# A hybrid backbone block on one Trainium2 core: attention pairs computed on 32-wide strips, keys transposed once per head pair, and filler gates split in four pieces

## The chip, the cores and the metric

The kernel runs on one core of a Trainium2 chip. Its time is device time in microseconds (us) for one execution of the whole block. A core has a matrix engine (PE, with its weight loads listed apart as PEld), a vector engine (DVE), a scalar engine (ACT), a general engine (POOL) and a sync engine (SP) that here only starts DMA transfers. Each engine takes its instructions strictly in the order of its own list and waits for the others through semaphores. "Before" is the median of three runs, 1084.16 us. A difference of 0.3% (3.25 us) or less is counted as no change.

## What is computed

One layer of a diffusion backbone: 512 latent tokens, 256 context tokens, width 1024, all in float32. A modulated RMS norm feeds one wide projection; two token mixers run on it (A: a gated delta rule, four heads; B: HGRN2, four heads; both scan in two directions, each from the final state of the context); the mixers' outputs are normed per head, gated, projected up, merged by sigmoid gates and projected out; then comes a SwiGLU feed-forward of width 2816. The two scans, per chunk:

```python
def gdn_chunk_scan(q, k, v, log_alpha, beta, s0, with_output):
    ...
    sol = lax.linalg.triangular_solve(a_mat, rhs, left_side=True, lower=True, unit_diagonal=True)
    ...
    k_end = k * jnp.exp(g_end[..., None] - g)[..., None]
    ...
    def step(s, xc):
        u_c = u_c - jnp.einsum('bhck,bhkv->bhcv', w_c, s)
        s_next = gam_end_c[..., None, None] * s + jnp.einsum('bhck,bhcv->bhkv', k_end_c, u_c)
        o = jnp.einsum('bhck,bhkv->bhcv', qg_c, s) + jnp.einsum('bhij,bhjv->bhiv', att_c, u_c)
        return s_next, o

def hgrn2_chunk_scan(q, k, v, log_f, s0, with_output):
    ...
    def step(s, xc):
        s_next = f_end_c[..., None] * s + jnp.einsum('bhck,bhcv->bhkv', k_end_c, v_c)
        pair = jnp.exp(jnp.where(incl[:, :, None], lg_c[:, :, :, None, :] - lg_c[:, :, None, :, :], -jnp.inf))
        att = jnp.einsum('bhik,bhjk,bhijk->bhij', q_c, k_c, pair)
        o = jnp.einsum('bhck,bhkv->bhcv', q_c * jnp.exp(lg_c), s) + jnp.einsum('bhij,bhjv->bhiv', att, v_c)
        return s_next, o
```

The kernel uses chunks of 128 tokens, not 64, and adds the triangular halves of both directions into one 128x128 attention matrix per chunk.

## The kernel before

**How the lists come about.** The program is written in a framework that gives every engine one fixed list of instructions, sorted by a priority that follows the order of writing. Tiles come from pools; a tag with `bufs=n` has n buffers, and an instruction that needs a buffer waits until the tile that held it n tiles ago has been read for the last time. PSUM has eight banks of 128x512 float32: two for the projections (tag `mm`), two for mixer B (`ha`), three for mixer A (`ga`), one for the filler gates (`fa`). A string, `PLAN`, says in which order pieces of the streams are written: `G0` and `G2` are mixer A's two pairs of heads, `H0` to `H3` mixer B's heads, `N` and `aT` pieces of the modulation product, `F` one filler gate, `X` the point after which the leftover gates and modulation pieces are written.

**Big products.** A weight matrix comes by DMA as `raw`. `split` makes of it a rounded part `hi` (ACT, L100) and the rest `lo` (DVE, L102); `mm3` (L110) multiplies hi by hi, hi by lo and lo by hi, three 128x512 matmuls for each 128 rows of weights. All projections, the gates and the feed-forward go this way.

**Filler gates.** There are 24 gate tiles of 128 columns. Nine are written by `gate_low` ahead of X: their matmuls (`pgate`) get a priority 1000 later than the place where they are written, so that they fall into gaps of the mixers. Each is made in two halves of four k-tiles (128x512 elements): one DMA of 256 KB, one cast, one subtraction, 12 matmuls. `hi` and `lo` of the pool `fl` have one buffer each, `raw` two; the finished gate goes by `gate_out` (an ACT copy and a DMA) to `gdram` in HBM.

**Mixer B (`hgrn`).** After its projections (`h_z`, `h_zv`) a head builds the attention matrix `AT` (128x4x128: four chunks side by side) level by level. Level 7 is the diagonal; levels 0 to 6 belong to b = 1, 2, 4, ..., 64: pairs whose tokens lie in the two halves of the same block of 2b tokens. Each level takes two exponentials on ACT (`E`, L511, and the first half of `kq`, L512), a product on DVE (L515, the second half of `kq`), `att`, and two updates of the running sums `K` and `L` on DVE. `att` multiplies for each of the four chunks all 128 keys with all 128 queries (L488, tile `pA` in a bank of `ha`), and then DVE copies with a mask only those pairs that belong to the level (L493, mask `lev`, 128 columns a level); level 7 is copied whole by ACT (L491). At the end `AT` is multiplied with the values into `po`.

**Mixer A (`gdn_pair`, two heads at once).** `gdn_front` makes convolved, normed keys `KTt` (key dimension on the partitions, six blocks of 128 tokens), queries and values. Then come decays and the matrices `N` and `aT`, and the inverse of the triangular matrices: a loop of 30 rounds on DVE (`p_o`, `p_Z`, L694 and L696) for 32-blocks, and solves with 32- and 64-wide matmuls (`pR`, `pX`, `pY`, L735 to L752; `pRb`, `pYb`, L760 to L770). Last come six steps, each for two heads and two directions; one of them (bank `pk`):

```python
                        nc.tensor.matmul(pk[:, P:2 * P], N[:, d, e, g, :], rt[:, :], start=True, stop=True)
                        u = rt
                        nc.scalar.activation(u[:, :], pk[:, P:2 * P], AF.Copy, scale=nbkv[:, g, d:d + 1])
                        ...
                            nc.tensor.transpose(pk[:, 2 * P:3 * P], KTt[:, g, :], ident)
                            nc.scalar.activation(kend[:, :], pk[:, 2 * P:3 * P], AF.Copy, scale=dec[:, d, 1, g, h:h + 1])
                            nc.tensor.matmul(pk[:, 2 * P:3 * P], kend[:, :], u[:, :], start=True, stop=True)
```

L792 is the product with `N`, L794 the ACT pass that makes `u` (named `p_s_r`, as it overwrites `rt`), L799 the transpose, L800 the ACT pass that makes `kend` (`p_s_ke`), L801 the product that updates the state, L804 (first step) the copy of the state `S`. The tag `blk` has three buffers and is used in turn by the convolution of the first two heads, the loop's tiles, the outputs `oa` and the normed outputs `on`. Other small matmuls named below: `column_sums` (L116: 128x32 weights at four column positions, one moving column).

## Time and profile before

| | |
|---|---|
| median of three runs | 1084.16 us (1082.39 to 1086.25) |
| profiled execution, its time | 1081.61 us |
| its span in the trace | 1079.6 us |
| granted PE clock, mean | 0.99 |
| PE, PEld busy | 1014.1 us (94%), 839.9 us (78%) |
| DVE, ACT busy | 656.5 us (61%), 554.5 us (51%) |
| POOL busy | 76.6 us (7%) |
| the chain that ended last, by engine | PE 60%, DVE 13%, DMA 9%, ACT 7%, issue 7% |
| moved by DMA | 122.07 MB, 113 GB/s on average |

Busy times add up each instruction's own time, overlaps within an engine counted once; matmuls are pipelined and their ends are modelled, so the distance from one start to the next says more about PE than a duration does. Each float32 matmul of the program with both operands in plain float32 leaves two records in the trace, a transpose one, and one in the hi/lo form (`mm3`) one. Three stretches of the span can be told apart: until about 95 us loads, norms and the first modulation; from 95 to 605 us both mixers, with the fillers in between; from 605 us on merge, output projection and feed-forward.

### The profile page before, as it was taken

What the parts mean: (1) busy time and instruction counts of PE and PEld (TensorE: products, weight loads), DVE (VectorE), ACT (ScalarE), POOL (GpSimd) and SP (SyncE); (2) the same over time, 40 slices, a digit from 0 to 9 for tenths busy, and PEclk for the clock granted to TensorE, in tenths of its full rate; (3) what the DMA queues carried; (4) which work ended last, traced back from release to release, by engine and by line L of the source; (5) the groups of instructions that cost most, each with busy time, mean ns of one, the idle gap of its engine ahead of it and who ended that gap; (6) DMA issues with size and microseconds to landing.
All of it is one profiled execution on the core that took longest, in us unless ns stands there. A gap on an engine that the chain in (4) does not pass through costs nothing.

```text
span 1079.6 us, 16501 instructions
## 1 busy us (share of the span) xinstructions
PE 1014.1 (94%) x6455; PEld 839.9 (78%) x6455; DVE 656.5 (61%) x1238; ACT 554.5 (51%) x1042; POOL 76.6 (7%) x133
## 2 busy tenths in 40 slices
PE   4999999979999999999999899999999999999996
PEld 2686788858897877789777688797888878888785
DVE  3336886789867967976797565776343433422524
ACT  3456578748976765887774643442222222221212
POOL 1010000320002022000201000010000000000000
PEclk8999999999999999999999999999999999999999
DMA  9953412122004213200738743455333323322222
GB/s 329 290 168 91 138 55 65 54 79 59 3 11 147 64 45 88 59 2 22 241 112 280 239 159 120 137 158 174 98 97 96 96 85 98 97 97 96 86 95 95
DMA packets 134529, 122.07 MB, mean 113 GB/s; under 512 B 5533, under 2 KB 110259, under 8 KB 134451
## 3 DMA queue, kind: packets, MB, share of 16 engines
q1 hardware_dynamic: 127715, 100.20, 29.9%
q0 software_dynamic: 4640, 17.30, 4.9%
q10 hardware_dynamic: 2096, 3.50, 0.9%
q8 instruction: 51, 0.84, 0.3%
q14 instruction: 27, 0.22, 0.1%
HBM read 110.51 MB, written 10.49 MB: 112 GB/s over the span
## 4 chain that ended last, share of the span: by engine, by line
PE 60%; DVE 13%; DMA 9%; ACT 7%; issue 7%; POOL 3%; SPq 0%; POOLq 0%; ACTq 0%; DVEq 0%
PE pf L110 20%; PE pfo L110 10%; PE pg L330 3%; PE pup L110 3%; PE h_z L110 3%; PE pgate L110 2%; DMA mwb<-in_mod_w_dram 2%; DVE lo L102 2%; DMA mwe<-in_mod_w_dram 2%; PE h_zv L110 2%; DMA ug<-gdram 1%; ACT hi L100 1%; DMA gdram<-gt 1%; PE p_s_pk L801 1%; PE g_k_zl L110 1%
## 5 line engine op out<-in xcount | busy, mean ns | idle before, releaser
L100 ACT CAST hi<-raw 128x1024 fp32r<-128x1024 f32 (+1 forms) x131 | 129.7, 991 | 279.9 <-PE pf L110 97.3
L102 DVE TENSOR_TENSOR lo<-raw,hi 128x1024 fp32r<-128x1024 f32 (+1 forms) x131 | 150.5, 1150 | 172.6 <-ACT hi L100 172.2
L110 PE MATMUL pf<-hhi,lo 128*128 128x512 f32 (+1 forms) x352 | 133.8, 380 | 0.8 <-DVE lo L102 0.8
L110 PE MATMUL pf<-hhi,hi 128*128 128x512 f32 (+1 forms) x352 | 133.8, 381 | 0.0
L110 PE MATMUL pf<-hlo,hi 128*128 128x512 f32 (+1 forms) x352 | 133.7, 380 | 0.0
L110 PEld LDWEIGHTS pf<-hhi,lo 128*128 128x128 f32 x352 | 66.2, 188 | 13.7 <-DVE lo L102 1.2
L110 PEld LDWEIGHTS pf<-hlo,hi 128*128 128x128 f32 x352 | 66.2, 188 | 12.5 <-DVE hlo L1042 0.2
L110 PEld LDWEIGHTS pf<-hhi,hi 128*128 128x128 f32 x352 | 66.1, 188 | 12.5
L110 PE MATMUL pfo<-lo,uh 128*128 128x512 f32 x176 | 68.8, 391 | 0.1
L110 PE MATMUL pfo<-hi,ul 128*128 128x512 f32 x176 | 68.5, 389 | 0.0
L110 PE MATMUL pfo<-hi,uh 128*128 128x512 f32 x176 | 67.9, 390 | 0.0
L110 PE MATMUL pgate<-hhi,lo 128*128 128x512 f32 x144 | 59.2, 412 | 6.5 <-DVE lo L102 6.5
L110 PE MATMUL pgate<-hhi,hi 128*128 128x512 f32 x144 | 59.2, 411 | 2.3 <-ACT hi L100 2.3
L110 PE MATMUL pgate<-hlo,hi 128*128 128x512 f32 x144 | 58.2, 404 | 0.0
L1098 DVE TENSOR_TENSOR sg<-sg,pf 128x512 f32<-128x512 f32 x22 | 15.1, 687 | 49.3 <-PE pf L110 49.3
L835 DVE SCALAR_TENSOR_TENSOR acc<-mwb,sc,acc 128x256 f32<-128x256 f32 x72 | 34.5, 484 | 12.4 <-DMA mwb<-in_mod_w_dram 11.2
L110 PEld LDWEIGHTS pfo<-lo,uh 128*128 128x128 f32 x176 | 33.0, 188 | 7.8 <-DVE lo L102 1.0
L110 PEld LDWEIGHTS pfo<-hi,uh 128*128 128x128 f32 x176 | 32.8, 188 | 7.4 <-ACT hi L100 0.7
L110 PEld LDWEIGHTS pgate<-hhi,lo 128*128 128x128 f32 x144 | 27.8, 193 | 13.8 <-DVE lo L102 8.9
L110 PE MATMUL h_z<-hhi,hi 128*128 128x512 f32 x96 | 38.1, 397 | 0.4 <-ACT abT L376 0.3
L110 PEld LDWEIGHTS pfo<-hi,ul 128*128 128x128 f32 x176 | 33.0, 188 | 6.8
L110 PE MATMUL h_z<-hhi,lo 128*128 128x512 f32 x96 | 38.0, 396 | 0.0
(443 smaller groups left out, 2498.3 us busy)
## 6 DMA issues: line engine op xcount, KB each, us to landing
raw<-in_ffn_w_in_dram SPq DMA_DIRECT2D x44, 512.0 KB, 3.7
raw<-in_w_in_dram SPq DMA_DIRECT2D x37, 512.0 KB, 3.7
raw<-in_ffn_w_out_dram SPq DMA_DIRECT2D x22, 512.0 KB, 3.6
mwb<-in_mod_w_dram POOLq DMA_DIRECT2D x18, 512.0 KB, 4.6
mw<-in_mod_w_dram SPq DMA_DIRECT2D x16, 512.0 KB, 6.0
mwe<-in_mod_w_dram POOLq DMA_DIRECT2D x7, 1024.0 KB, 6.1
gdram<-gt SPq DMA_DIRECT2D x24, 256.0 KB, 3.3
raw<-in_w_in_dram SPq DMA_DIRECT2D x18, 256.0 KB, 2.9
```

The costliest lines, as they stand in the source:

```text
L100: nc.scalar.copy(hi[:, :, :], raw[:, :, :])
L102: nc.vector.tensor_tensor(lo[:, :, :], raw[:, :, :], hi.bitcast(F32), op=ALU.subtract)
L110: nc.tensor.matmul(ps, a[u](k), b[v](k), start=(start and n == 0), stop=(stop and n == tot - 1))
L330: nc.tensor.matmul(pg0[i][:, :], u[:, P * i:P * i + P], v[:, d, :], start=(d == 0 and n == 0), stop=(d == KT - 1 and n == 2))
L801: nc.tensor.matmul(pk[:, 2 * P:3 * P], kend[:, :], u[:, :], start=True, stop=True)
L835: nc.vector.scalar_tensor_tensor(acc[:, :], mw[:, k - k0, :], sc[:, k:k + 1], acc[:, :], op0=ALU.mult, op1=ALU.add)
L1098: nc.vector.tensor_tensor(sg[:, :], sg[:, :], pgu[1][:, :], op=ALU.mult)
```

## The change

**Strips.** `att` no longer multiplies 128 keys by 128 queries. For levels 7 and 0 to 4 (blocks of at most 32 tokens) it multiplies, for each chunk, each 32 keys with the same 32 queries: 16 matmuls with 32x32 outputs at the four column positions of the array, all 128 rows in use. Their results stand as a strip of 128x(4x32). Level 7 is copied by ACT into a new tile `AD` (128x4x32), levels 0 to 4 by DVE under a mask of 32 columns a level. After level 4 four DVE copies move AD's diagonal blocks into `AT`. Level 5 (b = 32) multiplies 32 keys with the neighbouring 32 queries (`j ^ 1`), 16 matmuls, and four ACT copies of 32x4x32 write them straight into `AT`; level 6 does the same with 64x64, 8 matmuls and two ACT copies of 64x4x64. The mask `lev` shrinks from 128x896 to 128x160.

**Keys once per pair.** Between the inverse and the steps, for each head of a pair, six transposes of the keys go to two banks of `ga`, and two ACT copies (128x256, 128x512) bring them into `kt`, a tile with the tag `blk`; DVE makes `nbe`, the product of two small scale tables (128x12). In a step, the transpose and the pass for `kend` are gone: the pass after `N` is now `ue`, scaled by `nbe`, which goes into the state product with `kt`; `u` is made as well only where a latent chunk's output needs it (g >= 2).

**Filler gates in four pieces.** `gate_low` casts, subtracts and multiplies two k-tiles at a time (128x256); `hi` and `lo` have two buffers each, half as large. The DMAs stay two of 256 KB for each gate (tile `fraw`).

Counted over the program: ACT has 1040 instructions for 1006, DVE 1270 for 1240, PE's matmuls 5602 for 5266; POOL and SP keep their numbers, and SP's list is in the same order but for small shifts.

```diff
--- before.py
+++ after.py
@@ -24,6 +24,8 @@
 LEVELS = (1, 2, 4, 8, 16, 32, 64)
+NB = 32
+NSM = 5
@@ -37,7 +39,8 @@
     r, c = i[:, None], i[None, :]
     sq = np.concatenate(
         [(r == c), (r <= c), (r >= c), (r < c), (r > c)], axis=1).astype(np.float32)
-    lev = [(r // (2 * b) == c // (2 * b)) & (r // b != c // b) for b in LEVELS]
+    r, c = r % NB, c[:, 0:NB]
+    lev = [(r // (2 * b) == c // (2 * b)) & (r // b != c // b) for b in LEVELS[0:NSM]]
     return sq, np.concatenate(lev, axis=1).astype(np.float32)
 
@@ -142,11 +145,18 @@
         def gate_low(i, pool):
             ps = bank("fa", f"pgate{i}")
-            for k0 in (0, 4):
-                w = split([W_IN[P * k0:P * k0 + 4 * P, gcols[i]:gcols[i] + P]], 4, P, pool)
+            for k0 in range(0, KT, 2):
+                if k0 % 4 == 0:
+                    raw = pool.tile([P, 4, P], F32, name=f"fraw{i}{k0}", tag="raw", bufs=2)
+                    nc.sync.dma_start(raw[:, :, :], W_IN[P * k0:P * k0 + 4 * P, gcols[i]:gcols[i] + P].rearrange("(k p) f -> p k f", p=P))
+                part = raw[:, k0 % 4:k0 % 4 + 2, :]
+                hi = pool.tile([P, 2, P], F32R, name=f"fhi{i}{k0}", tag="hi", bufs=2)
+                nc.scalar.copy(hi[:, :, :], part)
+                lo = pool.tile([P, 2, P], F32R, name=f"flo{i}{k0}", tag="lo", bufs=2)
+                nc.vector.tensor_tensor(lo[:, :, :], part, hi.bitcast(F32), op=ALU.subtract)
                 tc.cur_priority += 1000
-                mm3(ps[:, :], [lambda k, t=t: t[:, k, :] for t in w], [lambda k, t=t: t[:, k0 + k, :] for t in lat], 4,
-                    start=(k0 == 0), stop=(k0 == 4))
+                mm3(ps[:, :], [lambda k, t=t: t[:, k, :] for t in (hi, lo)], [lambda k, t=t: t[:, k0 + k, :] for t in lat], 2,
+                    start=(k0 == 0), stop=(k0 == KT - 2))
                 tc.cur_priority -= 1000
             gate_out(i, ps, pool)
@@ -340,8 +350,8 @@
-            lev = cp.tile([P, 7 * P], U8, name="lev")
-            levf = s1.tile([P, 7 * P], F32, name="levf")
+            lev = cp.tile([P, NSM * NB], U8, name="lev")
+            levf = s1.tile([P, NSM * NB], F32, name="levf")
             nc.sync.dma_start(levf[:, :], T["lev"])
             nc.scalar.copy(lev[:, :], levf[:, :])
             mx = s1.tile([P, 4], F32, name="mx")
@@ -481,17 +491,31 @@
                     nc.vector.tensor_tensor(q[:, :], Z[:, 0:SEQ], sg[:, 0:SEQ], op=ALU.mult)
                 yield
             AT = hg.tile([P, 4, P], F32, name=n + "AT", tag="AT")
+            AD = hg.tile([P, 4, NB], F32, name=n + "AD", tag="AD")
             def att(kq, lvl):
+
+                w = 64 if lvl == 6 else NB
                 pA = bank("ha", f"{n}pA{lvl}")
                 for c in range(4):
-                    nc.tensor.matmul(pA[:, P * c:P * c + P], kq[:, 0, P * c:P * c + P], kq[:, 1, P * c:P * c + P],
-                                     start=True, stop=True)
+                    for j in range(P // w):
+                        kt0, qt0 = P * c + w * j, P * c + w * (j ^ (lvl in (5, 6)))
+                        nc.tensor.matmul(pA[w * j:w * j + w, w * c:w * c + w], kq[:, 0, kt0:kt0 + w], kq[:, 1, qt0:qt0 + w],
+                                         start=True, stop=True, tile_position=(0, w * j))
+                pAv = pA[:, 0:4 * w].rearrange("p (c i) -> p c i", i=w)
                 if lvl == 7:
-                    nc.scalar.copy(AT[:, :, :], pA.rearrange("p (c i) -> p c i", i=P))
+                    nc.scalar.copy(AD[:, :, :], pAv)
+                elif lvl < NSM:
+                    nc.vector.copy_predicated(AD[:, :, :], lev[:, NB * lvl:NB * lvl + NB].unsqueeze(1).to_broadcast([P, 4, NB]), pAv)
                 else:
-                    nc.vector.copy_predicated(AT[:, :, :], lev[:, P * lvl:P * lvl + P].unsqueeze(1).to_broadcast([P, 4, P]),
-                                              pA.rearrange("p (c i) -> p c i", i=P))
+                    for j in range(P // w):
+                        s = slice(w * j, w * j + w)
+                        nc.scalar.copy(AT[s, :, w * (j ^ 1):w * (j ^ 1) + w], pAv[s, :, :])
+                if lvl == NSM - 1:
+                    for j in range(P // NB):
+                        s = slice(NB * j, NB * j + NB)
+                        nc.vector.tensor_copy(AT[s, :, s], AD[s, :, :])
             kq = hg.tile([P, 2, SEQ], F32, name=n + "kqd", tag="kq", bufs=2)
             E = hg.tile([P, SEQ], F32, name=n + "Ed", tag="E")
@@ -772,6 +796,18 @@
 
             oa2 = gd.tile([P, 2, 4, P], F32, name=n + "oa", tag="blk", bufs=3)
+            kts = []
+            for e, (KTt, QTt, Vt, nbkv, eq) in enumerate(heads):
+                kt = gd.tile([P, 6, P], F32, name=f"{n}kt{e}", tag="blk", bufs=3)
+                for g0, cnt in ((0, 2), (2, 4)):
+                    pt = bank("ga", f"{n}kt{e}{g0}")
+                    for i in range(cnt):
+                        nc.tensor.transpose(pt[:, P * i:P * i + P], KTt[:, g0 + i, :], ident)
+                    nc.scalar.copy(kt[:, g0:g0 + cnt, :], pt[:, 0:P * cnt].rearrange("p (g k) -> p g k", k=P))
+                nbe = gd.tile([P, 6, 2], F32, name=f"{n}nbe{e}", tag="nbe", bufs=2)
+                nc.vector.tensor_tensor(nbe[:, :, :], nbkv, dec[:, :, 1, :, h0 + e].rearrange("p d g -> p g d"), op=ALU.mult)
+                kts.append((kt, nbe))
@@ -791,14 +827,15 @@
                                                            op0=ALU.mult, op1=ALU.subtract)
                         nc.tensor.matmul(pk[:, P:2 * P], N[:, d, e, g, :], rt[:, :], start=True, stop=True)
                         u = rt
-                        nc.scalar.activation(u[:, :], pk[:, P:2 * P], AF.Copy, scale=nbkv[:, g, d:d + 1])
+                        if step < 5:
+                            kt, nbe = kts[e]
+                            ue = gd.tile([P, P], F32, name=m + "ue", tag="ke", bufs=3)
+                            nc.scalar.activation(ue[:, :], pk[:, P:2 * P], AF.Copy, scale=nbe[:, g, d:d + 1])
                         if g >= 2:
+                            nc.scalar.activation(u[:, :], pk[:, P:2 * P], AF.Copy, scale=nbkv[:, g, d:d + 1])
                             nc.tensor.matmul(pk[:, 3 * P:], QTt[:, g - 2, :], S[t][:, :], start=True, stop=True)
                         if step < 5:
-                            kend = gd.tile([P, P], F32, name=m + "ke", tag="ke", bufs=3)
-                            nc.tensor.transpose(pk[:, 2 * P:3 * P], KTt[:, g, :], ident)
-                            nc.scalar.activation(kend[:, :], pk[:, 2 * P:3 * P], AF.Copy, scale=dec[:, d, 1, g, h:h + 1])
-                            nc.tensor.matmul(pk[:, 2 * P:3 * P], kend[:, :], u[:, :], start=True, stop=True)
+                            nc.tensor.matmul(pk[:, 2 * P:3 * P], kt[:, g, :], ue[:, :], start=True, stop=True)
                             if step == 0:
                                 S[t] = gd.tile([P, P], F32, name=m + "S", tag="S" + t)
                                 nc.scalar.copy(S[t][:, :], pk[:, 2 * P:3 * P])
```

What moves on the engines' lists, at three places. First PE, at the first levels of mixer B's last head (`H2`), where a gate fills in. Before:

```order
L488 MATMUL h_pA_5883<-h_kqd 128x128 x4
L488 MATMUL h_pA_5894<-h_kq_5889 128x128 x4
L459 MATMUL h_pv_6039<-sq,h_Zv 128x128 x4
L459 MATMUL h_pv_6045<-sq,h_Zv 128x128
L488 MATMUL h_pA_5907<-h_kq_5902 128x128 x4
L459 MATMUL h_pv_6045<-sq,h_Zv 128x128
```

And after (att's matmul is L504 there, mm3's L113):

```order
L113 MATMUL pgate_5826<-hhi,lo_5824 128x512
L504 MATMUL h_pA_6243<-h_kqd 32x32 x16
L504 MATMUL h_pA_6266<-h_kq_6261 32x32 x16
L113 MATMUL pgate_5826<-hhi,hi_5822 128x512
L113 MATMUL pgate_5826<-hlo,hi_5822 128x512
L113 MATMUL pgate_5826<-hhi,lo_5824 128x512
L113 MATMUL pgate_5826<-hhi,hi_5822 128x512
L113 MATMUL pgate_5826<-hlo,hi_5822 128x512
L113 MATMUL pgate_5826<-hhi,lo_5824 128x512
L504 MATMUL h_pA_6291<-h_kq_6286 32x32 x16
```

Four large matmuls of a level have become 16 small ones in one row; the transposes of the values (`h_pv`) have moved from here, and a gate's matmuls stand between the levels.

Second ACT, where the first pair goes from its inverse (the copy of `p_pYb`) into the steps, with a level of mixer B (`h_E`, `h_kq`) between. Before:

```order
L770 COPY p_N<-p_pYb_2742 64x6x64 x2
L794 ACTIVATE p_s_r<-p_s_pk,g_vec 128x128 x2
L512 ACTIVATE h_kq_3196<-h_K,lno 128x2x8x32
L800 ACTIVATE p_s_ke<-p_s_pk,dec 128x128 x2
L794 ACTIVATE p_s_r<-p_s_pk,g_vec 128x128
L804 COPY p_s_S<-p_s_pk 128x128
```

And after (L806 copies `kt`, L833 makes `ue`, L841 the state, L514 the copies into AT):

```order
L794 COPY p_N<-p_pYb_2782 64x6x64 x2
L806 COPY p_kt_2812<-p_kt_2813 128x256
L806 COPY p_kt_2812<-p_kt_2817 128x512
L806 COPY p_kt_2825<-p_kt_2826 128x256
L806 COPY p_kt_2825<-p_kt_2830 128x512
L833 ACTIVATE p_s_ue<-p_s_pk,p_nbe_2823 128x128 x2
L833 ACTIVATE p_s_ue<-p_s_pk,p_nbe_2836 128x128
L841 COPY p_s_S<-p_s_pk 128x128
```

Four copies of keys stand ahead of the first step's passes, and the two passes for `kend` between them are gone.

Third DVE, in the first pair's loop of 30 rounds, where the loop's two instructions alternate with a convolution (`g_q_acc`) and a gate's subtractions (`lo_1941`, `lo_1959`; then `flo`). Before:

```order
L694 TENSOR_TENSOR p_o_1915<-p_Z 128x150
L102 TENSOR_TENSOR lo_1941<-raw_1937,hi_1939 128x512
L696 TENSOR_TENSOR p_Z<-p_Z,p_o_1915 128x25x6
L605 SCALAR_TENSOR_TENSOR g_q_acc<-g_q_pad,cw,g_q_acc 128x540
L694 TENSOR_TENSOR p_o_1918<-p_Z 128x168
L102 TENSOR_TENSOR lo_2635<-raw_2631,hi_2633 128x1024
L696 TENSOR_TENSOR p_Z<-p_Z,p_o_1918 128x24x7
L694 TENSOR_TENSOR p_o_1921<-p_Z 128x184
L102 TENSOR_TENSOR lo_1959<-raw_1955,hi_1957 128x512
```

And after (the gate's subtraction is L156, the loop L718 and L720, the convolution L629):

```order
L720 TENSOR_TENSOR p_Z<-p_Z,p_o_1920 128x26x5
L156 TENSOR_TENSOR flo_1949<-fraw_1945,fhi_1947 128x256
L718 TENSOR_TENSOR p_o_1923<-p_Z 128x150
L156 TENSOR_TENSOR flo_1959<-fraw_1945,fhi_1957 128x256
L720 TENSOR_TENSOR p_Z<-p_Z,p_o_1923 128x25x6
L629 SCALAR_TENSOR_TENSOR g_q_acc<-g_q_pad,cw,g_q_acc 128x540
L718 TENSOR_TENSOR p_o_1926<-p_Z 128x168
L629 SCALAR_TENSOR_TENSOR g_q_acc<-g_q_pad,cw,g_q_acc 128x540
L720 TENSOR_TENSOR p_Z<-p_Z,p_o_1926 128x24x7
L156 TENSOR_TENSOR flo_1971<-fraw_1967,fhi_1969 128x256
```

The gate's two subtractions of 128x512 have become four of 128x256 spread over the same rounds, the first two ahead of where the first stood.

## Prediction

> **What bounds the kernel now.** I read the page's busy line and slices first, then busy time by stretch, then PE's waits where both mixers run, and last single places on the timeline, from one start to the next.
>
> ```profile
> span 1079.6 us, 16501 instructions
> ...
> PE 1014.1 (94%) x6455; PEld 839.9 (78%) x6455; DVE 656.5 (61%) x1238; ACT 554.5 (51%) x1042; POOL 76.6 (7%) x133
> ...
> PE   4999999979999999999999899999999999999996
> ```
>
> PE is the fullest engine, in nearly every slice; its clock is near full (0.99). Everything the change touches lies between 95 and 605 us. The next fence has that stretch, and inside it the steps of the first pair (265 to 345) and of the second (457 to 525); after PE and PEld each row gives DVE and ACT.
>
> ```profile
> 95.00:605.00 510.00, 481.20 (x3825) 409.40 (x3825) 401.25 (x844) 360.27 (x758) 58.32 (x97) 0.99 0.29 87
> ...
> 265.00:345.00 80.00, 75.98 (x803) 66.74 (x802) 60.69 (x136) 63.62 (x173) 6.12 (x7) 1.00 0.15 47
> 457.00:525.00 68.00, 64.07 (x744) 57.28 (x744) 48.05 (x121) 54.55 (x154) 7.35 (x8) 1.00 0.15 51
> ```
>
> PE stands still for 28.8 of the 510 us; DVE has 109 us free and ACT 150. So what leaves PE's list shortens the stretch, unless the chain of another engine shows up in its place. In the steps ACT is nearest to that: 80% busy in both (63.62 of 80, 54.55 of 68). PE's waits in that stretch (total, times, longest):
>
> ```profile
> PE pgate L110 <- DVE lo L102: 6.5, 5, 2.9
> PE p_pt L437 <- ACT p_on L434: 2.9, 2, 1.9
> PE p_pR L735 <- DVE p_T L703: 2.8, 2, 1.5
> ...
> PE pgate L110 <- ACT hi L100: 2.3, 4, 0.9
> ```
>
> The largest is the filler gate that waits for its own split: 6.5 + 2.3 = 8.8 us. Waits for mixer A's inverse (`p_pR`) stay where they are; no edit shortens the 30 rounds.
>
> **Strips.** A level as it is now, among the large matmuls of a projection:
>
> ```profile
> 364.60 0.39 PE L110 MATMUL h_zv<-hlo,hi 128*128 128x512 f32 x1
> 364.83 1.05 PE L488 MATMUL h_pA<-h_kq 128*128 128x128 f32 x8
> 365.64 0.48 PE L110 MATMUL h_zv<-hhi,lo 128*128 128x512 f32 x1
> 365.95 0.39 PE L110 MATMUL h_zv<-hhi,hi 128*128 128x512 f32 x1
> ```
>
> A large matmul starts 0.23 us after the one before it (364.60 to 364.83). From the level's start to the second large matmul after it pass 1.12 us; less 0.23, a level costs PE 0.89 us, for 8 records (two for each of its four matmuls). A strip level has 16 matmuls, so 32 records. Before has no such shape; the nearest row is the column sums, whose weights are 128x32 at four column positions, though with one moving column instead of 32. Next to them stand 32x32 and 64x64 pieces of the inverse:
>
> ```profile
> 133.28 0.39 PE L110 MATMUL pgate<-hlo,hi 128*128 128x512 f32 x1
> 133.60 0.58 PE L116 MATMUL g_k_pn<-ones,g_k_acc 128*32 128x1 f32 x48
> 134.10 0.50 PE L110 MATMUL g_k_zl<-hhi,hi 128*128 128x512 f32 x1
> 134.44 0.39 PE L110 MATMUL g_k_zl<-hlo,hi 128*128 128x512 f32 x1
> ...
> 457.09 0.62 PE L735 MATMUL p_pR<-p_T,p_N 32*32 32x32 f32 x48 [1.47 <-DVE p_T L703]
> 457.64 0.50 PE L110 MATMUL h_z<-hhi,lo 128*128 128x512 f32 x1
> ...
> 283.05 0.87 PE L760 MATMUL p_pRb<-p_X,p_N 64*64 64x64 f32 x24
> 283.85 0.60 PE L488 MATMUL h_pA<-h_kq 128*128 128x128 f32 x3
> ```
>
> 48 column-sum records cost 1.16 us from 133.28 to 134.44, less two large matmuls (0.46): 0.70 us, changes of shape included. 48 records of 32x32 take 0.55 us to the next start (11 ns each), 24 of 64x64 take 0.80 us (33 ns each). For 32 records the low end is 0.55 x 32/48 = 0.37 us, with no change of shape beyond what that row has; the high end is the 64x64 price, 32 x 33 ns = 1.06 us. I take 0.58 us, between two thirds of 0.70 and all of it, since the weights' height and the four column positions are those of the column sums and the 32 columns are those of `p_pR`. That saves 0.31 us a level, in 28 levels (seven of eight, four heads) 8.7 us; by the ends a saving of 14.6 or a loss of 4.8. Level 6 has 8 matmuls, 16 records at 33 ns = 0.53 us, which saves 0.36 us in each of four heads, 1.4 us.
>
> The Trainium skill's page "TensorE: Matmul & The Clock Gate", section "Wait — 56ns, not 53.3ns?", says that starts never come closer than about 25 ns however small the matmul is. By that, an estimate from the page, 32 records would be 0.80 us, and with what a change of shape costs the level would save nothing. The rows above disagree for matmuls on different parts of the array: 48 starts in 0.55 us are 11 ns apart.
>
> **Strips on ACT and DVE.**
>
> ```profile
> L493 DVE COPY_PREDICATED h_AT<-lev,h_pA 128x512 f32<-128x512 uint8 x28 | 20.6, 734 | 2.4 <-PE h_pA L488 2.2 <-PE h_pv L459 0.2
> L491 ACT COPY h_AT<-h_pA 128x512 f32<-128x512 f32 x4 | 2.3, 582 | 0.4 <-PE h_pA L488 0.4
> L549 ACT COPY h_kt<-h_pkb 128x128 f32<-128x128 f32 x8 | 2.2, 272 | 0.4 <-PE h_pkb L546 0.4
> L615 ACT COPY g_v_acc<-g_v_pad 128x256 f32<-128x256 f32 x4 | 1.6, 400 | 0.0
> L1042 DVE TENSOR_TENSOR hlo<-hf,hhi 128x256 fp32r<-128x256 f32 x16 | 6.7, 422 | 2.4 <-ACT hhi L1041 2.2
> ```
>
> DVE loses 20.6 us of masked copies and gets 20 of 128x128 and 16 of 32x128, at some 0.27 us (by L549, ACT's copy of that size) 9.7 us. ACT gets 24 small copies at most that size, 6.5 us, and its level-7 copy falls from 2.3 to 1.1. Both lie beside PE's work, and the group of masked copies waits for PE (2.2 us), not PE for it. The shorter DVE pass lets a bank of `ha` go 0.46 us earlier in 20 levels, and DVE's two updates that follow start earlier; PE hardly waited there, so I take 1 us (ends 0 and 5: half of 20 x 0.46).
>
> **Keys once per pair.** 40 transposes become 24, starts 0.11 us apart:
>
> ```profile
> 288.79 0.27 PE L799 MATMUL p_s_pk<-sq,g_KT 128*128 128x128 f32 x1
> 288.90 0.39 PE L488 MATMUL h_pA<-h_kq 128*128 128x128 f32 x2
> ```
>
> 16 x 0.11 = 1.8 us off PE. ACT's passes, by their groups:
>
> ```profile
> L800 ACT ACTIVATE p_s_ke<-p_s_pk,dec 128x128 f32<-128x128 f32 x40 | 14.4, 370 | 5.3 <-PE p_s_pk L799 4.7
> L794 ACT ACTIVATE p_s_r<-p_s_pk,g_vec 128x128 f32<-128x128 f32 x48 | 17.3, 370 | 7.5 <-PE p_s_pk L792 6.7
> ```
>
> 40 `ue` take the place of 40 `kend`, 16 `u` go (5.8 us of busy time). The chain of a step keeps its length: product, pass, product. New at the head of a pair's steps are 12 transposes and four copies, 2 x 0.40 + 2 x 0.58 = 1.97 us of ACT, which in ACT's list stand ahead of the first `ue`, behind the copy of `p_pYb`; the first state products wait for them, and the six pieces of the first step on both heads behind those. In the gap PE has the first step's products with `N` and levels of mixer B. The ends are 0 and 1.97 for each pair; I take 1 each, 2 us, and give back 1 us for 16 passes fewer in stretches where ACT is 80% busy (ends 0 and 5.8). The small product for `nbe` is 4 DVE instructions nobody waits for before the first `ue`. SP and POOL keep their lists.
>
> **Gates in four pieces.**
>
> ```profile
> L100 ACT CAST hi<-raw 128x512 fp32r<-128x512 f32 x18 | 11.1, 615 | 6.8 <-DVE p_o L694 5.0 <-PE pgate L110 1.7
> L102 DVE TENSOR_TENSOR lo<-raw,hi 128x512 fp32r<-128x512 f32 x18 | 12.4, 688 | 3.1 <-ACT hi L100 2.9 <-issue 0.2
> ...
> 225.21 0.40 PE L110 MATMUL pgate<-hlo,hi 128*128 128x512 f32 x1
> 228.49 0.80 PE L110 MATMUL pgate<-hhi,lo 128*128 128x512 f32 x1 [2.89 <-DVE lo L102]
> ...
> 237.46 0.43 PE L116 MATMUL g_q_pn<-ones,g_q_acc 128*32 128x1 f32 x32 [1.21 <-ACT g_q_acc L631]
> ```
>
> Cast and subtraction of a piece fall from 0.615 + 0.688 to 0.400 + 0.422 us (L615, L1042), 0.48 us sooner, and the next piece can be split while the last one is multiplied. Busy time rises, ACT by 36 x 0.400 - 11.1 = 3.3 us and DVE by 36 x 0.422 - 12.4 = 2.8. Of 8.8 us of waits the longest, 2.9, brings nothing: at 237.46 PE waits for a convolution on the same engines anyway, and would only wait longer there. Of the other 5.9 us I take half, 3 (ends 0 and 5.9).
>
> **Sum.** PE's list: 8.7 + 1.4 + 1.8 = 11.9 us. I pass on 85% of it, since PE stands still for 6% of the stretch and some of what is saved will turn into waits for ACT: 10.1 (ends 50% and all). With 1 (DVE), 3 (gates), 1 (fewer passes) and against 2 (keys) the gain is 13.1 us. The profiled execution took 1081.61 us, 2.55 below the median: 1068.5 for it, 1071 for the median. 0.3% (3.25 us) is about what a measurement can tell here from no change.
>
> **Rivals.** *More comes through* (0.20): strips at 0.47 us (11.8), all 1.4 and 1.8, all 5.9 of the gates, 5 from DVE, keys at nothing: 26 us, 1058. For it: PE is on nearly every stretch of the path. Against it: levels and steps have chains of their own. *PE's saving is not on the path* (0.14): mixer chains over ACT and DVE set the length, a third of 11.9 arrives, gates bring nothing, keys cost 2: 1082, between 1079 and 1084. For it: 28.8 us of waits exist, at the inverse above all. Against it: the waits at `h_pA` are almost nil. *Strips are no cheaper* (0.07), the change not doing what it says: at 33 ns a record, 4.8 us lost against 3.2 + 3 + 2 - 2 gained, 1083. The rows at 457.09 speak against it. This is where the rule of the Trainium skill's page "TensorE: Matmul & The Clock Gate" would end. *ACT takes over* (0.09), slower: PE's saving is not passed on, since ACT's list in the steps carries the extra work, 24 copies (6.5), `kt` (3.9) and the casts' 3.3, less 5.8 + 1.2, 6.7 us net; if on top both pairs wait the whole of 1.97 at their start and nothing is hidden, 1084 + 6.7 + 3.9 - 3 = 1092. It decides when ACT is over about 95% busy in the two rows of the steps, where it has 29.8 us free; that is why it stays small. My forecast has the remaining 0.50, with 1064 to 1079 as its own range.
>
> The range: 1057 to 1082 leaves out about 2 in 10, at the top those two that end at no change or slower. Faster by over 0.3% (below 1080.9): 0.50 + 0.20 + 0.10 of the third case = 0.80; within 0.3%: the rest of it and the strips, 0.11; slower: 0.09.
>
> **What would show it.** Level: from strip start to the second large matmul behind it 0.8 us instead of 1.12. Masked copies near 0.27 us. PE's records more by some 690 (352 more matmuls with two each, 16 transposes fewer), its span between 95 us and the merge shorter by 11 to 14 us, the feed-forward untouched. Waits of `pgate` on `lo` and `hi` together below 6 us. `p_kt` copies ahead of `ue` with PE idle under 1 us at each pair's start. I am wrong if strip records start 25 ns or more apart, if ACT is above 95% in the steps, or if waits for `p_T`, `p_on` or `h_on` grow by what PE gave.

## The result: 0.8% slower, outside the range

The changed kernel takes 1089.51 us (median of 12 runs, 1086.6 to 1095.3), the kernel before 1082.64 us beside it (12 runs): a ratio of 1.0083, 95% interval 1.0063 to 1.0104. Forecast were 1071 us and a range that ended at 1082. The profiled execution took 1089.22 us, its span is 1087.5 us.

The page after, its busy line and the slices of PE and its clock:

```profile
span 1087.5 us, 17970 instructions
...
PE 1009.7 (93%) x7143; PEld 827.4 (76%) x7143; DVE 646.2 (59%) x1268; ACT 557.3 (51%) x1076; POOL 74.6 (7%) x133
...
PE   4998999989899999869989799999999999999996
...
PEclk9999999999999999979989999999999999999999
```

PE and DVE have less to do than before, and yet the span is 7.9 us longer. Slice 18 of PE is at 6 where it was at 9 before: PE stands still there. By stretch, the second pair's steps and what follows them:

```profile
265.00:345.00 80.00, 75.34 (x993) 63.38 (x992) 56.94 (x144) 62.73 (x178) 5.16 (x7) 1.00 0.18 54
...
457.00:525.00 68.00, 57.92 (x787) 51.60 (x786) 41.48 (x112) 50.92 (x141) 4.86 (x6) 0.90 0.08 28
525.00:605.00 80.00, 72.11 (x594) 56.59 (x593) 64.35 (x130) 52.02 (x103) 9.80 (x12) 0.96 0.66 211
```

Between 457 and 525 us PE is busy for 57.92 us (64.07 before) at a granted clock of 0.90 (1.00). PE's waits over the whole span:

```profile
PE p_pR L759 <- DVE p_T L727: 5.5, 2, 4.3
PE h_pA L504 <- DVE h_kq L537: 5.4, 6, 1.7
...
PE p_pY L765 <- ACT p_T L762: 4.9, 3, 3.9
...
PE pgate L113 <- DVE lo L105: 2.3, 1, 2.3
```

The gates' waits went as forecast, from 8.8 us to 3.0 (2.3 for `lo`, 0.4 for `hi`, 0.3 for `flo`). In their place stand waits for the inverse (`p_pR` 2.8 before, now 5.5; `p_pY` 2.6, now 4.9) and for the levels' factor `kq`, for which PE hardly waited before (0.3 us in the group of its matmuls).

The way there, as starts on PE or DVE, before and after: first product of the first pair's steps 285.6 and 291.0 us (5.4 later, of which 2 had arisen ahead of 95 us, where almost nothing was changed, and the transposes and copies of the keys made 2.6); last product of these steps 328.9 and 329.6 (the steps gave 4.7 back); second loop's start 418.1 and 425.4; its end 453.1 and 465.6; first product of the second steps 471.2 and 486.8; last one 512.7 and 521.2 (7.1 given back); the up-projections' first product 600.1 and 605.0; end 1079.6 and 1087.5. So of the 7.9 us between these two executions 3 are added behind 600 us, where nothing was changed (PE's waits for `x` there are 5.2 us, before 3.6), and 2 ahead of 95 us; in the stretch of the mixers 2.7 us remain, though PE has less to do there. Inside it most is lost between the first steps and the second pair's steps.

Two places show why. Ahead of the second loop, PE now takes gates before the second pair's projections: their first matmul starts at 332.9 us instead of 321.2, and by then 144 gate matmuls have run instead of 107; 37 of them at 0.23 us are 8.5 us. Inside the second loop 5.2 us are lost. DVE there, before and after (start, duration):

```profile
418.05 0.21 DVE L694 TENSOR_TENSOR p_o<-p_Z 128x30 f32<-128x30 f32 x1 [1.16 <-POOL p_Z L689]
...
451.81 0.73 DVE L493 COPY_PREDICATED h_AT<-lev,h_pA 128x512 f32<-128x512 uint8 x1
...
453.13 2.10 DVE L702 STREAM_TRANSPOSE p_T<-p_Z 128x1024 f32<-128x1024 f32 x1
```

```profile
425.35 0.21 DVE L718 TENSOR_TENSOR p_o<-p_Z 128x30 f32<-128x30 f32 x1 [1.16 <-POOL p_Z L713]
...
449.02 0.30 DVE L510 COPY_PREDICATED h_AD<-lev,h_pA 128x128 f32<-128x128 uint8 x1
449.22 0.39 DVE L720 TENSOR_TENSOR p_Z<-p_Z,p_o 128x228 f32<-128x228 f32 x1
449.52 0.69 DVE L537 TENSOR_TENSOR h_kq<-h_q,h_E 128x512 f32<-128x512 f32 x1
450.12 0.42 DVE L156 TENSOR_TENSOR flo<-fraw,fhi 128x256 fp32r<-128x256 f32 x1
450.46 0.38 DVE L718 TENSOR_TENSOR p_o<-p_Z 128x220 f32<-128x220 f32 x1
450.76 0.69 DVE L539 TENSOR_TENSOR h_K<-h_K,h_L 128x512 f32<-128x512 f32 x1
451.36 0.39 DVE L720 TENSOR_TENSOR p_Z<-p_Z,p_o 128x220 f32<-128x220 f32 x1
...
465.61 1.93 DVE L726 STREAM_TRANSPOSE p_T<-p_Z 128x1024 f32<-128x1024 f32 x1
```

Between the rounds of the loop stand masked copies, products and updates of mixer B's head H3: five levels, where before there was one. The loop, which everything of the second pair waits for, takes 40.3 us instead of 35.1. What PE does meanwhile:

```profile
463.19 0.28 PE L113 MATMUL h_z<-chi,lo 128*128 128x256 f32 x1
464.62 0.46 PE L504 MATMUL h_pA<-h_kq 128*32 128x32 f32 x32 [1.15 <-DVE h_kq L537]
469.38 0.86 PE L759 MATMUL p_pR<-p_T,p_N 32*32 32x32 f32 x48 [4.30 <-DVE p_T L727]
474.10 0.26 PE L765 MATMUL p_pY<-p_T 32*32 32x32 f32 x2 [3.86 <-ACT p_T L762]
```

Nothing else stands in PE's list between these rows; PE idles for 9 us in 11. Before, projections (`h_z`) followed there on `p_pR` at once (457.64 us).

### The profile page after: what moved, and what is told of

Read it like the earlier page. It is cut to its first block, busy times and chain, and to the rows that moved or that the text cites. A ratio compares the mean times of both kernels' runs of the same rounds, so it can differ in the third digit from the quotient of the medians.

```text
span 1087.5 us, 17970 instructions
## 1 busy us (share of the span) xinstructions
PE 1009.7 (93%) x7143; PEld 827.4 (76%) x7143; DVE 646.2 (59%) x1268; ACT 557.3 (51%) x1076; POOL 74.6 (7%) x133
## 4 chain that ended last, share of the span: by engine, by line
PE 62%; DVE 14%; ACT 8%; DMA 7%; issue 5%; POOL 2%; SPq 0%; POOLq 0%; DVEq 0%; ACTq 0%
PE pf L113 20%; PE pfo L113 10%; PE pup L113 3%; PE pg L340 3%; PE pgate L113 2%; PE h_z L113 2%; DMA mwb<-in_mod_w_dram 2%; PE h_zv L113 2%; DMA gdram<-gt 1%; DVE p_o L718 1%; PE g_q_zl L113 1%; DVE p_Z L720 1%; DVE lo L105 1%; PE g_k_zl L113 1%; PE g_v_zl L113 1%
## 5 line engine op out<-in xcount | busy, mean ns | idle before, releaser
L103 ACT CAST hi<-raw 128x1024 fp32r<-128x1024 f32 x113 | 118.6, 1050 | 273.5 <-PE pf L113 101.7
L105 DVE TENSOR_TENSOR lo<-raw,hi 128x1024 fp32r<-128x1024 f32 x113 | 138.2, 1223 | 167.5 <-ACT hi L103 167.3
L113 PE MATMUL pf<-hhi,lo 128*128 128x512 f32 (+1 forms) x352 | 133.8, 380 | 0.9 <-DVE lo L105 0.9
L113 PE MATMUL pf<-hhi,hi 128*128 128x512 f32 (+1 forms) x352 | 133.8, 381 | 0.0
L113 PE MATMUL pf<-hlo,hi 128*128 128x512 f32 (+1 forms) x352 | 133.7, 380 | 0.0
L113 PEld LDWEIGHTS pf<-hhi,lo 128*128 128x128 f32 x352 | 66.2, 188 | 13.9 <-DVE lo L105 1.4
L113 PEld LDWEIGHTS pf<-hlo,hi 128*128 128x128 f32 x352 | 66.2, 188 | 12.6 <-DVE hlo L1079 0.2
L113 PEld LDWEIGHTS pf<-hhi,hi 128*128 128x128 f32 x352 | 66.1, 188 | 12.3
L113 PE MATMUL pfo<-lo,uh 128*128 128x512 f32 x176 | 68.8, 391 | 0.1
L113 PE MATMUL pfo<-hi,ul 128*128 128x512 f32 x176 | 68.5, 389 | 0.0
L113 PE MATMUL pfo<-hi,uh 128*128 128x512 f32 x176 | 67.9, 390 | 0.0
L872 DVE SCALAR_TENSOR_TENSOR acc<-mwb,sc,acc 128x256 f32<-128x256 f32 x72 | 34.3, 483 | 15.6 <-DMA mwb<-in_mod_w_dram 14.5
L113 PE MATMUL h_z<-hhi,hi 128*128 128x512 f32 x96 | 39.0, 406 | 1.2 <-ACT h_Z L479 0.8
L113 PEld LDWEIGHTS pfo<-lo,uh 128*128 128x128 f32 x176 | 33.0, 188 | 7.7 <-DVE lo L105 1.0
L113 PE MATMUL h_z<-hhi,lo 128*128 128x512 f32 x96 | 38.5, 401 | 0.0
L113 PE MATMUL h_z<-hlo,hi 128*128 128x512 f32 x96 | 38.4, 400 | 0.0
L113 PEld LDWEIGHTS pfo<-hi,uh 128*128 128x128 f32 x176 | 32.8, 188 | 7.4 <-ACT hi L103 0.7
L113 PEld LDWEIGHTS pfo<-hi,ul 128*128 128x128 f32 x176 | 33.0, 188 | 6.8
L113 PE MATMUL pgate<-hhi,lo 128*128 128x512 f32 x72 | 29.2, 410 | 2.3 <-DVE lo L105 2.3
L113 PE MATMUL pup<-yh,hi 128*128 128x512 f32 x64 | 26.0, 406 | 5.4 <-DVE x L1013 5.2
L113 PE MATMUL pgate<-hhi,flo 128*128 128x512 f32 x72 | 29.8, 414 | 0.4 <-DVE flo L156 0.3
```

Source lines behind the costliest of these rows:

```text
L103: nc.scalar.copy(hi[:, :, :], raw[:, :, :])
L105: nc.vector.tensor_tensor(lo[:, :, :], raw[:, :, :], hi.bitcast(F32), op=ALU.subtract)
L113: nc.tensor.matmul(ps, a[u](k), b[v](k), start=(start and n == 0), stop=(stop and n == tot - 1))
L872: nc.vector.scalar_tensor_tensor(acc[:, :], mw[:, k - k0, :], sc[:, k:k + 1], acc[:, :], op0=ALU.mult, op1=ALU.add)
```

## The experiments

**The three parts alone.** Each is the kernel before with one part of the diff, or the change without the gates.

```diff
 # e1, and e4 with e2 besides
+                        nc.tensor.matmul(pA[w * j:w * j + w, w * c:w * c + w], ..., tile_position=(0, w * j))
 # e2
+                nc.vector.tensor_tensor(nbe[:, :, :], nbkv, dec[:, :, 1, :, h0 + e].rearrange("p d g -> p g d"), op=ALU.mult)
+                kts.append((kt, nbe))
 # e3
+            for k0 in range(0, KT, 2):
```

> The kernel before with the strips alone. Theory A (order): the strips let the last big head of mixer B (H3) run ahead, its levels get into DVE's list between the 30 rounds of the second pair's inverse (three levels here, five in the full change), and all nine fillers stand ahead of that inverse, so PE idles there. Then the second loop takes 3 to 5 us more than the 38.8 us of before, the waits of p_pR and p_pY together are 6 us or more, and the time is 1079 to 1085. Rival K (keys): the loss comes from kt at the head of each pair's steps; then the strips alone bring their 8 to 12 us, 1071 to 1075. Rival G (gates): the loss comes from fillers that take PE early; then this kernel gains 8 to 12 us too.

> The kernel before with the keys transposed once per pair alone. Rival K: the copies at the head of the steps cost 2 to 2.6 us in each pair and the shorter steps give less back, so 1085 to 1088. Theory A: the steps get 4 to 5 us shorter in each pair and give back more than the head costs, 1077 to 1082, with the second loop at 38 to 40 us. Rival G: no loss here either.

> The kernel before with the gates in four pieces alone. Rival G: fillers come early, the second pair's front starts 4 us or more later and the time is 1086 to 1090. Theory A: the order of the second loop has no levels of mixer B in it here, so no loss, 1079 to 1083, and the waits of pgate fall from 8.8 to under 4 us.

> The change without the gate split. Theory A: three levels in the second loop instead of five, so about half of the loss goes: 1080 to 1085. Rival G: all of the loss goes and the gain of strips and keys shows, 1069 to 1074. Rival K: still slower than before, 1086 or more.

Measured: strips 1.0101 (1.0067 to 1.0135; 1092.8 us), keys 1.0025 (1.0007 to 1.0044; 1086.1 us), gates 1.0024 (1.0000 to 1.0048; 1084.2 us), strips and keys 1.0076 (1.0051 to 1.0102; 1091.8 us), with before at 1081.6 us. No part gains, and the strips lose most, 11 us. That speaks for Theory A's part, but its number was too small, and one of its signs failed: with the strips alone the second loop is longer (39.0 us, counted as above, for 35.1), yet the waits of `p_pR` and `p_pY` together are 4.8 us, not 6 or more. Rival K hit the numbers of keys and of strips and keys; as the main cause it falls, and G with it, because the strips lose without them. The gates came out between the forecasts of A and G. By their ratios keys and gates alone are no change (within 0.3%; the keys' medians lie 4.5 us apart), where I forecast gains. The parts add up to 1.5%, the whole loses 0.8%: they are not independent.

**Strips and order apart.** Every engine's list can be held to an order that another kernel got, by chaining its instructions (an edge for the order of issue, no wait):

```diff
+    told = zlib.decompress(base64.b85decode(ORDER)).decode().split("\n")
+    ...
+                    tc.add_manual_dep(i, last, mybir.DependencyInfo(mybir.DependencyClass.NoSync, mybir.DependencyReason.DATA), reason="order")
```

> The strips alone, with every engine's list held to the order of before: each strip level stands where the 128x128 level stood, chunk by chunk, the masked copy where the masked copy stood; only the six copies of ACT for levels 5 and 6 are left to the scheduler. Theory A (order): the strips are cheaper and only the order that the scheduler makes of them costs; then the 10 us that PE saves come through in large part, 1070 to 1077. Rival S (strips): something in the strips themselves costs (their matmuls, the clock, the extra copies on ACT); then this is slow as well, 1086 to 1095.

> The instructions of before, with every engine's list held to the order that the strips alone got. Theory A: slow although no instruction differs from before, 1090 to 1100. Rival S: as fast as before, within 1079 to 1085.

> The strips alone, PE's list held to the order of before, the other engines' lists left to the scheduler. If it is PE's list that costs (fillers ahead of the second pair's projections), 1070 to 1077; if it is DVE's (levels of mixer B between the rounds of the second loop), 1086 to 1094; rival S also says 1086 or more.

> The strips alone, the lists of DVE and ACT held to the order of before, PE's list left to the scheduler. If DVE's list is what costs, 1070 to 1077; if PE's is, 1086 to 1094; rival S says 1086 or more.

Measured: strips in the order of before 1.0086 (1.0058 to 1.0115); before in the strips' order 1.0123 (1.0093 to 1.0154); strips with only PE's list of before 1.0156 (1.0120 to 1.0192), with only DVE's and ACT's 1.0104 (1.0068 to 1.0140). Of the first two, each theory hits one and misses one. The order by itself costs 13 us with not one instruction changed (e6). But the strips are nearly as slow in the order of before (8 us) as in their own (11 us; the intervals overlap). So for the strips themselves the two orders differ by some 3 us, and either something in the strips costs too, or the order of before does not suit them. No single list of before brings the time back: e7 and e8 are as slow as rival S said, and neither the forecast for PE's list nor that for DVE's came true.

What an order does can be read in the second loop. Its length goes, roughly, with the number of masked copies, one for each level, that stand between its rounds:

| masked copies in the second loop | kernels | loop, us |
|---|---|---|
| 0 | e2, e3 | 33.4, 32.3 |
| 1 or 2 | before, e5, e7, e8 | 35.1, 34.4, 35.0, 34.3 |
| 3 | e1, e4, e6 | 39.0, 38.7, 40.5 |
| 5 | the change | 40.3 |

In e6, the instructions of before:

```profile
426.08 0.21 DVE L930 TENSOR_TENSOR p_o<-p_Z 128x30 f32<-128x30 f32 x1 [1.44 <-POOL p_Z L925]
...
466.63 2.07 DVE L938 STREAM_TRANSPOSE p_T<-p_Z 128x1024 f32<-128x1024 f32 x1
```

And in e6 too 144 gate matmuls run ahead of the second pair's projections, which start at 333.9 us. But a long loop is not the whole loss: e7 and e8 are among the slowest with short ones.

e5 and before have the same rows on PE but for the levels, so they can be laid side by side: between 278 and 302 us, at the first pair's steps, e5 falls 4 us behind. ACT there, in e5:

```profile
293.32 0.38 ACT L1047 ACTIVATE p_s_r<-p_s_pk,g_vec 128x128 f32<-128x128 f32 x1
293.57 1.05 ACT L742 COPY h_AT<-h_pA 32x128 f32<-32x128 f32 x4
294.64 0.63 ACT L764 ACTIVATE h_E<-h_L 128x512 f32<-128x512 f32 x1
295.30 0.27 ACT L1057 COPY p_s_S<-p_s_pk 128x128 f32<-128x128 f32 x1
...
299.14 0.37 ACT L1047 ACTIVATE p_s_r<-p_s_pk,g_vec 128x128 f32<-128x128 f32 x1
299.39 0.74 ACT L742 COPY h_AT<-h_pA 64x256 f32<-64x256 f32 x2
300.16 1.06 ACT L773 ACTIVATE h_QG<-h_L 128x1024 f32<-128x1024 f32 x1
301.24 0.37 ACT L1053 ACTIVATE p_s_ke<-p_s_pk,dec 128x128 f32<-128x128 f32 x1
```

ACT goes from pass to pass without a gap. Level 5's copies (1.05 us) stand ahead of the state's copy `p_s_S`, for which the next products wait, and level 6's (0.74 us) ahead of a pass for `kend`. From the pass `p_s_r` to that `p_s_S` 1.98 us go by; the same two are 0.77 us apart in before.

**Copies, work and idling.** All in the order of before:

```diff
 e9:  + the strip matmul twice             e12: + the 128x128 level matmul twice
 e10: - nc.scalar.copy(AT[s, :, ...        + nc.vector.tensor_copy(AT[s, :, ...
 e11: - kq = hg.tile([P, 2, SEQ], F32      + kq = hg.tile([P, 2, SEQ], mybir.dt.bfloat16
```

> The strips in the order of before, each strip matmul issued twice into the same place (the second overwrites the first with the same numbers), so PE has some 9 us more to do in the levels. Theory C (clock): with the strips PE does too little in places, the granted clock halves more often (27 us at half clock between 95 and 610 us, before 7), and that costs more than the strips save; then doubling does not make it slower, 1082 to 1090 with a clock at or above that of the single strips (0.982). Theory W (work): PE's work counts, and doubling costs 5 to 9 us, 1095 to 1100.

> The strips in the order of before, with the copies of levels 5 and 6 on DVE in the place of the masked copies they replace, and not on ACT. Theory T (ACT takes over): these copies stand in ACT's list ahead of the passes of the steps (1.05 and 0.74 us in the first pair's steps) and make the strips slow; then 1076 to 1084. Theory C: nothing much changes, 1086 to 1092, since PE's idle places and its clock stay.

> The kernel before in its own order, with the two factors of each level (kq) kept in bfloat16, so that the level's matmuls take a quarter of PE's time (about 21 us less in all); ACT and DVE do the same number of passes, the pairs are only less exact. Theory W: 85% of it comes through, 1062 to 1068. Theory C: PE's list is not what ends the stretch, and PE idles more; no gain, 1080 to 1092, at a lower clock (under 0.987).

> The kernel before in its own order, with each 128x128 level matmul issued twice, 28.7 us more for PE. Theory W: 1105 to 1111. Theory C with slack on PE: well under that, 1085 to 1097, with a clock of 0.990 or more.

Measured: strips twice 1.0119 (1.0073 to 1.0164; 1093.1 us); levels 5 and 6 by DVE 1.0042 (1.0017 to 1.0066; 1085.2 us); pairs in bfloat16 1.0017 (0.9995 to 1.0039; 1082.0 us); pairs twice 1.0198 (1.0150 to 1.0245; 1100.0 us). Of the forecasts only Theory C's for e11 was hit; e9, e10 and e12 came out between the two theories.

e10 takes half of the strips' loss away, 1085.2 us against e5's 1090.3 (the intervals overlap a little): the copies on ACT do not seem to lie beside other work. Place by place the traces show about half of these 5 us where the theory has them: the two pairs' steps take 44.2 and 42.9 us, in e5 45.6 and 44.1, in before 43.3 and 41.5. e11 is the plainest of all. A level there, next to a projection:

```profile
369.53 0.39 PE L342 MATMUL h_zv<-hlo,hi 128*128 128x512 f32 x1
369.76 0.40 PE L721 MATMUL h_pA<-h_kq 128*128 128x128 bf16 x4
369.96 0.48 PE L342 MATMUL h_zv<-hhi,lo 128*128 128x512 f32 x1
370.28 0.40 PE L342 MATMUL h_zv<-hhi,hi 128*128 128x512 f32 x1
```

By the working of the prediction it costs 0.52 - 0.23 = 0.29 us for 0.89, 19 us less in 32 levels, nearly twice what the strips save, with the passes of ACT and DVE as long as before; and the time stays where it was. Theory W falls: cheaper levels bring nothing here. Not all of that need be slack, for the profiled e11 also has 20 us more at half clock than before (below). Dearer levels are not free: e12 has 29 us more work and takes 19 us longer; the strips twice, 9 us more work, take about 3 us more than e5, within its uncertainty.

**What is left: the clock, and mending the whole.**

```diff
 e13: keys alone, lists as before       e16: all three parts, levels 5 and 6 by DVE, lists as before
 e14: the change, levels 5 and 6 by DVE e15, e17, e18: e10, e11 and before, with
+                warm(pR, 5 if e == 0 else 0)     # likewise ahead of pY and pYb
+                nc.tensor.matmul(ps[:, :], hhi[:, k % KT, 0:P], hhi[:, k % KT, :], start=True, stop=True)
```

> The keys once per pair alone, all lists held to the order of before (ue where u stood; only the transposes into kt, their copies and nbe are left to the scheduler). Theory A (order): the steps get some 5 us shorter in each pair and this comes through in part when nothing else moves, 1074 to 1080. Rival K (the copies at the head of the steps cost as much): 1081 to 1087.

> The whole change with the copies of levels 5 and 6 on DVE instead of ACT, the order the scheduler's own. Theory T (ACT takes over): 4 to 6 us less than the change, 1083 to 1087. If the order swallows it: 1088 to 1094.

> The strips with levels 5 and 6 by DVE in the order of before (1085.2 us, clock 0.9845), and in front of the products that wait in the inverse (p_pR, p_pY, p_pYb) 15 large matmuls per pair that nobody reads, 3.4 us, less than PE idles there. Theory C (clock): they keep the clock at full speed around 270 to 290 and 465 to 475 us, clock 0.988 or more, and the time falls to 1079 to 1083. If the clock only follows the idling and costs nothing: 1085 to 1090.

> All three parts (levels 5 and 6 by DVE) with the lists held to the order of before. If the order is what is left of the loss once ACT is relieved: 1072 to 1080. If idling PE and its clock take what the parts save: 1081 to 1088.

> The bfloat16 pairs in the order of before (1081.95 us, clock 0.983; PE has 21 us less to do) with the same 15 unread matmuls per pair in the waits of the inverse. Theory C: what PE's lighter levels save was lost to the halved clock; with the clock held (0.988 or more) some of it shows, 1074 to 1079. If the stretch ends on ACT and DVE whatever the clock is: 1080 to 1084.

> The control: before with the same unread matmuls. Its clock is already at full speed around the inverse (1.00 at 265 to 285 and 455 to 475 us), so they can only cost: 1080 to 1084, no change within 0.3%. Were it 2 us or more faster, the matmuls would help in some other way than by the clock of these places.

Measured: e13 1.0081 (1.0052 to 1.0109), e14 1.0135 (1.0107 to 1.0163), e15 1.0020 (1.0004 to 1.0037), e16 1.0087 (1.0058 to 1.0116), e17 1.0011 (0.9992 to 1.0031), e18 1.0005 (0.9987 to 1.0022).

e15, e18 and the second forecast for e17 were hit; e13, e14 and e16 came out above both of theirs. Moving 24 copies to DVE, worth 5 us with the order held, made the scheduler write other lists, and the whole change went from 1089.5 to 1095.5 us (e14). And the order of before is good for before alone: the keys lose 0.25% in the order that the scheduler gives them and 0.81% in that of before (e13), and all parts together (e16) are as slow there as in their own. This weakens e5 too: a held order can itself be what costs.

The clock: in 5 us steps, before spends some 7 us at half clock between 95 and 610 us, the changed kernel, e5, e10 and e11 some 27 us each, and e6, with the instructions of before, 24 us. The unread matmuls of e15 bring e10's 27 us down to 7; e10 and e15 in the first and second inverse (PE's busy time first, granted clock third from the end):

```profile
265.00:285.00 20.00, 16.21 (x463) 12.77 (x463) 15.11 (x27) 16.28 (x38) 0.90 (x2) 0.83 0.06 18
...
455.00:475.00 20.00, 15.82 (x463) 13.28 (x461) 13.89 (x23) 16.82 (x39) 0.74 (x1) 0.91 0.07 20
```

```profile
265.00:285.00 20.00, 17.91 (x469) 13.81 (x468) 14.03 (x22) 17.08 (x40) 0.74 (x1) 1.00 0.02 4
...
455.00:475.00 20.00, 18.56 (x514) 14.60 (x513) 14.27 (x29) 18.63 (x47) 0.75 (x1) 1.00 0.02 4
```

The clock is full again and the median falls from 1085.2 to 1082.6 us, as theory C said; but the intervals overlap, and the same matmuls bring nothing to e11 (e17: 1083.6 against 1082.0), whose clock they did not lift: in the profiled e17 it is 0.982 and still drops at 280, 344 and 365 us. The control e18 moves nothing. So the half clock is worth some 2.5 us, by the medians, where it was removed; that it explains more is not shown, and for e11 it stays open.

No kernel tried beats the one before; e11, e17 and e18 equal it.

## Why the prediction was wrong

**The first step that failed is the sum's "I pass on 85% of it".** It took PE's 94% and 28.8 us of standing still for a bound. e11 measures that share: 19 us off PE's levels, no gain (1.0017), its lower clock included. With none of the 10.1 us passed on, the sum would still end at 1081 us for the median; the other 8 us up to 1089.5 are losses that it had at nothing, and they follow below. The view that says so was there and I did not take it by stretch: the chain of waits. Its shares for 265 to 300 us of the kernel before:

```profile
by line: PE h_pA L488 10.8%; PE p_s_pk L792 7.2%; ACT p_N L710 6.7%; ACT p_N L750 6.4%; PE p_s_pk L801 6.4%; ACT h_kq L512 5.9%; DVE p_T L703 5.6%; ACT p_X L712 5.5%; PE p_s_pk L789 5.3%; issue 5.2%; PE p_pYb L766 5.0%; PE p_s_pk L799 3.9%;
```

Added up row by row from 95 to 605 us, PE has 214 of the 510 us of that chain, and `h_pA` some 11 of the 28.5 us (32 x 0.89) that its levels cost. And a matmul of 128x512 is written as busy for 0.39 us while the next starts after 0.23. Counted at the distance from start to start (0.23 us for 128x512, 0.12 for 128x256, 0.11 for a 128x128 record, the small ones at the prices of the prediction), the records of that stretch add up to some 450 us. By this estimate, which leaves changes of shape out, PE has about twice the 28.8 us of slack.

**The term that was missing is the order.** I showed the lists at three places and read none in the second loop, where five of H3's levels for one now stand between the rounds, nor PE's list ahead of the second pair's projections. The order of the strips' kernel alone is worth 13 us on unchanged instructions (e6); how much of the change's own loss it makes is not shown, since with the strips in place the two orders differ by 3 us (e1, e5). The sentence that the waits for mixer A's inverse stay where they are fell with it: `p_pR` went from 2.8 to 5.5 us, `p_pY` from 2.6 to 4.9.

**Strips on PE: right.** A level costs what was forecast:

```profile
450.06 0.40 PE L113 MATMUL pgate<-hlo,fhi 128*128 128x512 f32 x1
450.38 0.46 PE L504 MATMUL h_pA<-h_kq 128*32 128x32 f32 x32
450.77 0.50 PE L113 MATMUL pgate<-hhi,flo 128*128 128x512 f32 x1
451.11 0.39 PE L113 MATMUL pgate<-hhi,fhi 128*128 128x512 f32 x1
```

From 450.06 to 451.11 are 1.05 us, less two large matmuls 0.59; forecast were 0.58. (Counted from the level's own start, as in the forecast's sign, it is 0.73 us for 0.8.) Two levels in a row show the strips by themselves:

```profile
446.88 0.46 PE L504 MATMUL h_pA<-h_kqd 128*32 128x32 f32 x32 [2.73 <-ACT h_kqd L525]
447.16 0.49 PE L504 MATMUL h_pA<-h_kq 128*32 128x32 f32 x32
```

32 records start within 0.28 us, 9 ns each, or 18 ns for each of the level's 16 matmuls; the other 0.31 us are changes of shape. The 25 ns between starts that the Trainium skill's page "TensorE: Matmul & The Clock Gate" (section "Wait — 56ns, not 53.3ns?") gives as a floor do not hold for these matmuls, which lie at four column positions of the array. The rival that strips are no cheaper was wrong.

**Strips on ACT and DVE: sizes right, the second term at nothing wrong.**

```profile
L510 DVE COPY_PREDICATED h_AD<-lev,h_pA 128x128 f32<-128x128 uint8 x20 | 6.1, 303 | 1.8 <-PE h_pA L504 1.7
L518 DVE COPY h_AT<-h_AD 32x128 f32<-32x128 f32 x16 | 3.5, 217 | 0.3
...
L514 ACT COPY h_AT<-h_pA 32x128 f32<-32x128 f32 x16 | 4.1, 255 | 0.9 <-PE h_pA L504 0.7
L514 ACT COPY h_AT<-h_pA 64x256 f32<-64x256 f32 x8 | 2.9, 364 | 0.2
```

DVE got 9.6 us (9.7 forecast), ACT 7.0 (6.5). But I costed ACT's copies at nothing, beside PE's work. In the steps they stand in front of the passes that the state waits for, and taking them off ACT brings about 5 us in the order of before (e5 against e10), of which the steps show half; in the change's own order they could not be told from the new lists (e14). That is what the rival "ACT takes over" named, with 0.09; its deciding point, 95% busy, was the wrong one: ACT was busy for 51 of 68 us and 63 of 80. An engine can delay a chain by what stands in its list ahead of the chain's link, however idle it is on average.

**Keys.** The transposes and copies at the head, 1 us for each pair in the forecast, cost 2.6 and 2.0 us. The four copies and what surrounds them on ACT, in the first pair:

```profile
289.14 0.95 ACT L794 COPY p_N<-p_pYb 64x384 f32<-64x384 f32 x2
290.11 1.70 ACT L806 COPY p_kt<-p_kt 128x256 f32<-128x256 f32 x4
291.71 0.37 ACT L833 ACTIVATE p_s_ue<-p_s_pk,p_nbe 128x128 f32<-128x128 f32 x1
```

The steps got shorter by much more than the 1 us I took (43.3 to 38.6 us, 41.5 to 34.4; with the keys alone 36.6 and 35.6), yet alone the keys cost 0.25%: what the steps gave, the stretch after them did not take (from the last product to the up-projections 101.1 us in e2, 87.4 before). Nor do the missing passes by themselves shorten the steps: with the lists held (e13) they take 44.1 and 41.4 us.

**Gates.** The waits fell as forecast, in e3 to 2.3 us in all; yet alone the part costs 0.24% instead of bringing 3 us. So the waits removed were worth no time.

Open: how the change's 6.9 us divide between order, copies and clock; what the strips still lose in the order of before with the copies off ACT (1.0042), beyond the 2.5 us that e15 may have shown; and how much of e11's missing gain is slack and how much is its lower clock.

## What to carry to other kernels

Cut work where the chain of waits of that stretch has it, and take its share there as the most that can come: a full busy row of a pipelined engine hides slack. When a scheduler writes the lists, a change is also a new order; hold the order to tell the two apart, in both directions, since an order that suits one kernel can slow the other; and read the lists in the longest serial loop first. Price a small pass on a half-idle engine by what stands behind it in that engine's list.

## What the hardware showed that was not expected

A PE that stands still can be slowed down. At the changed kernel's second inverse, where PE waits 1.15, 4.3 and 3.9 us between 463 and 474 us, the granted clock was at half from 465.9 to 479.6 us; in e5 waits of 0.6 and 1.2 us between 358 and 364 us were followed by 3.4 us at half clock from 365.1. Not every such wait had this effect: in before, waits of 1.3 and 0.8 us at the first inverse left the clock at 1.00. Between 95 and 610 us it made 7 us in before and 20 to 31 us in the change and in e1 to e8; cheaper work on PE is not needed for it, as e6 (24 us) shows. Matmuls that nobody reads, placed in the waits, held the clock at 1.00 around both inverses in e15, not in e17, and cost nothing measurable (e18, 1.0005).
